# Two value products of 256 columns joined to one of 512 in a matmul-bound decoder trunk

## The chip, the cores and the metric

The kernel runs on one core of a Trainium2 chip. The metric is the device time of one execution in microseconds (us). Before the change it was run three times: median 2363.1, lowest 2362.75, highest 2363.84.

## The reference: what is computed

A decoder trunk of two layers on 512 tokens of width 1024. A layer is a half-step SwiGLU, then a token mixing of three kinds of attention side by side, then another half-step SwiGLU, each between RMS norms. Only the mixing is touched:

```python
u = _rmsnorm(h, mix_pre_g[l])
proj = u @ w_in[l]
q_sb, k_sb, v_sb, q_fx, k_fx, v_fx, f_logit, q_mem = jnp.split(proj, split_at, axis=-1)
o_sb = _stick_breaking_attention(heads(q_sb), heads(k_sb), heads(v_sb))
log_f = jax.nn.log_sigmoid((f_logit + b_forget[l]).astype(jnp.float32)).transpose(0, 2, 1)
o_fx = _forgetting_attention(heads(q_fx), heads(k_fx), heads(v_fx), log_f)
o_mem = _memory_attention(heads(q_mem), heads(k_mem), heads(v_mem))
g_sb, g_fx, g_mem = jnp.split(jax.nn.sigmoid(u @ w_gate[l] + b_gate[l]), 3, axis=-1)
merged = g_sb * (o_sb @ w_br_sb[l]) + g_fx * (o_fx @ w_br_fox[l]) + g_mem * (o_mem @ w_br_mem[l])
h = h + _rmsnorm(merged @ w_out[l], mix_post_g[l])
```

Stick-breaking ("sb") and forgetting ("fx", in the code "fox") attention have 8 heads of 64 each, so their values are 512 columns of `w_in` each: columns 1024 to 1535 and 2560 to 3071. The eight forget logits are the columns 3072 to 3079, directly behind the forgetting values. Forgetting attention adds the running sum of log_f to its scores.

## The kernel before, in words

**Three matmuls for one.** Every fp32 operand is split in a high part h (a rounding copy on ScalarE) and a low part l (a subtraction on VectorE), `split` (line 179). A product is then three matmuls, h·h, h·l and l·h: `mm3` (lines 203 to 207), or lines 1096 to 1098 in `vproj`. Weights come through a DMA on SP's queue into one of two "raw" buffers, and are split into one of four buffer pairs "wh" and "wl". Such a piece of weights is a `Unit` (line 232), of at most 128 x 1024 elements; `Unit.load` (line 252) fetches and splits it.

**The queue.** The big products are jobs in a `Queue` (line 350). A job is a list of units and a generator; each step of the generator emits one group of three matmuls. When a job starts, its units are loaded, and then those of the jobs behind it, until four units are counted (`load_ahead`, line 391). The attention heads are chains of small steps with waits between them (a score product, a softmax on ScalarE and VectorE, transposes on TensorE, a value product). `Queue.weave` (line 437) interleaves one head with steps of jobs, by an estimated time of the matmuls (`PE_US`, line 229), and a limit says up to which job the fillers of a head may go (lines 1474 and 1475). Between these, the framework orders instructions by their place in the program and by what is ready; the transposes and value products of a head are pinned behind what stands before them on TensorE.

**PSUM.** There are eight banks of 128 x 512: four of tag "z" (scores and transposes) and four of tag "mm" (all other products, among them a head's value product, line 1186). A bank is free again once its readers are done.

**Values.** A token tile is 128 tokens; there are four (NT), and eight 128-row blocks of the width (ND). For values the token tile is the stationary operand and the weight's columns are the moving one. Per layer `project_v` (line 1373) queues four jobs, each for the two pairs of heads in 256 columns:

- stick-breaking pairs 0 and 1, then pairs 2 and 3, and forgetting pairs 0 and 1: `v_half` (line 1345), two units of four blocks and 256 columns; it takes a bank for two token tiles, 256 columns each, and evacuates 512 columns at once.
- forgetting pairs 2 and 3 with the forget logits behind them: `v_gates` (line 1326), three units of up to three blocks and 264 columns; a bank for each token tile, evacuated as 256 columns of values and 8 of logits (line 1343).

The values lie in tiles of tag "v", six buffers, two tiles for each job. `forget_cumsum` (line 1285), queued behind forgetting's first k, transposes and sums the logits.

**The order of a layer's mixing.** The memory heads come first, with the first stick-breaking q, k and values as fillers; then eight stick-breaking heads, then eight forgetting heads (pairs 2, 3, 0, 1). The fillers are, in the queue's order: the next head pair's q and k, a merge (two gate products of the width, `pg`, and two branch products, `pb`), and the values of the pair after next (lines 1457 to 1467). `project_v(0, 2)` is queued in the first turn, `project_v(1, 2)` in the third and `project_v(1, 0)` in the fifth. In layer 0 these jobs run at 465 to 479 us, 556 to 571 us and 649 to 663 us of the trace; layer 1 has the same order some 1173 us later.

Of the kernel before, what the change touches and what calls it, by code (L numbers as in the profile page):

```python
# [9 lines left out]
F32 = mybir.dt.float32  # L10
# [8 lines left out]
P = 128  # L19
# [4 lines left out]
def kernel(  # L24
# [38 lines left out]
    nc = tc.nc  # L63
    _, S, D = x.shape
    M = mem.shape[1]
    L = w_in.shape[0]
    NT = S // P
    ND = D // P
    MT = M // P
    HD = 64  # L70
    NP = 4
    NH = 8
# [31 lines left out]
    def stile(shape, tag, name, dt=F32R):  # L104
        return sb.tile(shape, dt, tag=tag, bufs=BUFS[tag], name=name)
# [4 lines left out]
    def pbank(tag, name):  # L110
        return ps.tile([P, S], F32, tag=tag, bufs=4, name=name)
# [67 lines left out]
    def split(h_ap, l_ap, src, scale=None, later=False):  # L179

        if scale is None:
            both = [nc.scalar.copy(h_ap, src)]  # L182
            make = lambda: nc.vector.tensor_tensor(l_ap, src, h_ap.bitcast(F32), ALU.subtract)  # L183
        else:
            both = [nc.scalar.activation(h_ap, src, AF.Copy, scale=scale)]  # L185
            make = lambda: nc.vector.scalar_tensor_tensor(l_ap, src, scale, h_ap.bitcast(F32), ALU.mult, ALU.subtract)  # L186
        if later:
            return make
        both.append(make())
        if Q.pinned:  # L190
            for ins in both:
                tc.keep_in_program_order(ins)
# [10 lines left out]
    def mm3(pt, lh, ll, rh, rl, start, stop, free=False):  # L203

        nc.tensor.matmul(pt, lh, rh, start=start, stop=False, skip_group_check=free)  # L205
        nc.tensor.matmul(pt, lh, rl, start=False, stop=False, skip_group_check=free)  # L206
        nc.tensor.matmul(pt, ll, rh, start=False, stop=stop, skip_group_check=free)  # L207
# [14 lines left out]
    def quad_act(ts):  # L222

        return lambda k, c=FULL: (ts[k // 4][:, k % 4, 0, c], ts[k // 4][:, k % 4, 1, c])
# [4 lines left out]
    PE_US = 1 / 2370.0  # L229


    class Unit:


        def __init__(self, src, k0, nk, c0, ncol, name, scale=None):
            self.tags, self.place = ("wh", "wl"), "raw"
            self.src, self.k0, self.nk, self.c0, self.ncol, self.name, self.scale = src, k0, nk, c0, ncol, name, scale
            self.h = self.raw = None
# [5 lines left out]
        def fetch(self):  # L244
            if not self.waits():
                return
            Q.took(self.place, 1)
            self.raw = stile([P, self.nk, self.ncol], self.place, "raw_" + self.name, F32)
            nc.sync.dma_start(self.raw[:], self.src[self.k0 * P:(self.k0 + self.nk) * P, self.c0:self.c0 + self.ncol]
                              .rearrange("(k p) c -> p k c", p=P))  # L250
# [13 lines left out]
        def split_from(self, raw, **how):  # L264
            shape = [P, self.nk, self.ncol]
            if isinstance(self.tags, str):
                both = stile([P, 2] + shape[1:], self.tags, "w_" + self.name)
                self.h, self.l = both[:, 0], both[:, 1]
            else:
                self.h = stile(shape, self.tags[0], "wh_" + self.name)[:]  # L270
                self.l = stile(shape, self.tags[1], "wl_" + self.name)[:]
            return split(self.h, self.l, raw, scale=self.scale, **how)

    class BlockUnit(Unit):

# [68 lines left out]
    def wpair(src, ktiles, c0, name, scale=None):  # L344

        return [Unit(src, k, min(4, ktiles - k), c0, 256, f"{name}_{k}", scale) for k in range(0, ktiles, 4)]
# [116 lines left out]
    Q = Queue()  # L463
# [622 lines left out]
    def vproj(units, act, tiles, name):  # L1086

        pt = pbank("mm", name)
        for i, t in enumerate(tiles):
            o = pt[:, i * 256:(i + 1) * 256]  # L1090
            ts_ = slice(t * P, (t + 1) * P)
            for un in units:
                for k in range(un.nk):
                    ah, al = act(un.k0 + k)
                    first = i == 0 and un.k0 + k == 0
                    nc.tensor.matmul(o, ah[:, ts_], un.h[:, k], start=first, stop=False)
                    nc.tensor.matmul(o, ah[:, ts_], un.l[:, k], start=False, stop=False)
                    nc.tensor.matmul(o, al[:, ts_], un.h[:, k], start=False, stop=(i == 1 and un.k0 + k == ND - 1))  # L1098
                    yield 768 * PE_US
        return pt  # L1100
# [182 lines left out]
    FOX = (2, 3, 0, 1)  # L1283
# [24 lines left out]
    def mixing(l, src, ks, vs, rest, dst):  # L1308
# [4 lines left out]
        act = lambda k, c=FULL: quad_act(src.us)(k, c)  # L1313
        st, marks = {}, {}
# [11 lines left out]
        def v_gates(br, c, un):  # L1326

            st["fl"] = sb.tile([P, NT, NH], F32, tag="fl", bufs=1, name=f"fl{l}")
            for t in range(NT):
                if t % 2 == 0:  # L1330
                    vt = stile([P, 4, 4, HD], "v", f"v{l}_{br}_{c}_{t // 2}")
                    st.setdefault(("v", br, c), []).append(vt)
                pt = pbank("mm", f"pv{l}_{br}_{c}_{t}")
                for un1 in un:
                    for k in range(un1.nk):
                        kk = un1.k0 + k
                        ah, al = act(kk, slice(t * P, (t + 1) * P))
                        mm3(pt[:, :un1.ncol], ah, al, un1.h[:, k], un1.l[:, k], kk == 0, kk == ND - 1)
                        yield 3 * un1.ncol * PE_US
                e = 2 * (t % 2)  # L1340
                split(vt[:, e:e + 2, 0:4:3, :], vt[:, e:e + 2, 1:3, :],
                      pt[:, :4 * HD].rearrange("p (a e c) -> p a e c", a=2, e=2))
                nc.vector.tensor_copy(st["fl"][:, t], pt[:, 4 * HD:4 * HD + NH])

        def v_half(br, c, un):
            for i in range(NT // 2):

                vt = stile([P, 4, 4, HD], "v", f"v{l}_{br}_{c}_{i}")
                st.setdefault(("v", br, c), []).append(vt)
                pt = yield from vproj(un, act, (2 * i, 2 * i + 1), f"pv{l}_{br}_{c}_{i}")  # L1350
                split(vt[:, :, 0:4:3, :], vt[:, :, 1:3, :], pt[:].rearrange("p (a e c) -> p a e c", a=4, e=2))
# [21 lines left out]
        def project_v(br, p):  # L1373

            base = br * 1536 + 1024 + p // 2 * 2 * P
            if (br, p) == (1, FOX[0]):
                un = [Unit(w_in[l], k, min(3, ND - k), base, 2 * P + NH, f"v{l}_{br}_{p}_{k}")
                      for k in range(0, ND, 3)]
                Q.add(un, lambda: v_gates(br, p // 2, un))
            else:  # L1380
                un = wpair(w_in[l], ND, base, f"v{l}_{br}_{p}")
                Q.add(un, lambda: v_half(br, p // 2, un))

# [64 lines left out]
        for c in range(2):  # L1448
            un = wpair(w_in[l], ND, 3080 + c * 256, f"qm{l}_{c}")
# [3 lines left out]
        heads, fox = [(0, p) for p in range(NP)] + [(1, p) for p in FOX], []  # L1453
        project(*heads[0])
        project_v(*heads[0])
        marks[heads[0]] = len(Q.jobs)
        for i, (br, _) in enumerate(heads):
# [203 lines left out]
    for l in LAYERS:  # L1661
        i, mn = 3 * l, []
        ma = ffn(l, subs[i], ffn1_w_gate, ffn1_w_up, ffn1_w_down, subs[i + 1], f"a{l}", "v",
                 park[2 * l] if l else None, PLAN, lambda l=l, mn=mn: mem_norm(l, mn))
        rest = mem_kv(l, mn, *kvs[l])
        mb = mixing(l, subs[i + 1], *kvs[l], rest, subs[i + 2])
        if l == 0:
            Q.weave(begin(), ma["first"])
            more_constants()
        else:  # L1670
            for part, units in zip(mc["next"], (ma["early"][:2], ma["early"][2:])):
                part.extend(units)
            for un in ma["early"][2:]:
                un.place = "v"
            boundary(mc, mc["end"], ma["first"])
        boundary(ma, ma["end"], mb["first"])
        mb["run"]()
        mc = ffn(l, subs[i + 2], ffn2_w_gate, ffn2_w_up, ffn2_w_down, subs[i + 3], f"c{l}", "o", park[2 * l + 1], PLAN)
        for part, units in zip(mb["next"], (mc["early"][:2], mc["early"][2:])):
                part.extend(units)  # L1680
        boundary(mb, mb["end"], mc["first"])
# [25 lines left out]
```

## Time and profile before

| what | us |
|---|---|
| median of three runs | 2363.1 |
| the profiled execution | 2364.23 |
| span of its trace | 2362.5 |
| TensorE (PE) busy | 2341.4, 11719 matmuls |
| VectorE (DVE) busy | 1798.8 |
| ScalarE (ACT) busy | 1510.6 |

PE is the matmul part of TensorE, PEld its weight load, DVE VectorE, ACT ScalarE, POOL GpSimd, SP the engine that issues most transfers. An instruction is named by its line, its engine and the names of the tiles that it writes and reads ("pv<-wh_v,us_a": into a bank of values, from the value weights' high part and the normed activations). The profile's shares, groups and waits are of one execution. A matmul's record is the time from its start to its end, and the records of consecutive matmuls overlap; the distance of two starts tells what one costs in a stream.

### The profile page before, as it was taken

The numbers are of one execution on the slowest core, as the hardware profiler recorded it, in microseconds if no ns is written. First come the engines' busy times: TensorE is split into PE (matmuls) and PEld (weight loads), VectorE is DVE, ScalarE is ACT, GpSimd is POOL, SyncE is SP. The second block draws the span as 40 slices with busy tenths as digits, with TensorE's granted clock in tenths as the row PEclk, the third lists the DMA queues.
The fourth block names the chain that finished last, engine by engine and source line by source line (L and its number), as shares of the span: only waits on it lengthen the run. The fifth ranks groups of instructions, "written<-read, shape, count | busy, mean of one in ns | idle before, by whom it ended". The sixth has DMA issues, their size and how long they took to land.

```text
span 2362.5 us, 31122 instructions
## 1 busy us (share of the span) xinstructions
PE 2341.4 (99%) x11719; PEld 1980.5 (84%) x11719; DVE 1798.8 (76%) x2358; ACT 1510.6 (64%) x2305; POOL 75.4 (3%) x134
## 2 busy tenths in 40 slices
PE   9999999999999999999999999999999999999998
PEld 7788889888888888878888878888888888888887
DVE  8877877577777688878788778766767766887785
ACT  6777465576766556774556765655777665567744
POOL 0000000000111000000000000000001100000000
PEclk9999999999999999999999999999999999999999
DMA  5667454223323555674646665532323235566744
GB/s 205 183 178 216 147 190 139 81 83 88 90 72 107 188 188 162 194 187 154 221 131 195 200 178 167 198 108 72 95 76 99 72 124 188 171 186 175 220 140 143
DMA packets 299754, 354.98 MB, mean 150 GB/s; under 512 B 78266, under 2 KB 192978, under 8 KB 299604
## 3 DMA queue, kind: packets, MB, share of 16 engines
q1 hardware_dynamic: 299508, 352.97, 49.1%
q8 instruction: 92, 1.51, 0.3%
q14 instruction: 58, 0.48, 0.1%
q0 software_dynamic: 96, 0.03, 0.0%
HBM read 319.39 MB, written 16.78 MB: 142 GB/s over the span
## 4 chain that ended last, share of the span: by engine, by line
PE 85%; DVE 4%; DMA 4%; ACT 4%; issue 2%; SPq 0%; POOL 0%; DVEq 0%; ACTq 0%
PE pg L206 4%; PE pg L205 4%; PE pg L207 4%; PE pda L206 3%; PE pda L207 3%; PE pda L205 3%; PE pdc L206 2%; PE pdc L207 2%; PE pdc L205 2%; PE pb L206 2%; PE pb L207 2%; PE pb L205 2%; PE pq L206 1%; PE pq L205 1%; PE pk L207 1%
## 5 line engine op out<-in xcount | busy, mean ns | idle before, releaser
L205 PE MATMUL pg<-us_a,wh_wg 128*128 128x512 f32 x384 | 150.9, 393 | 0.0
L207 PE MATMUL pg<-us_a,wl_wg 128*128 128x512 f32 x384 | 149.8, 390 | 0.0
L206 PE MATMUL pg<-us_a,wh_wg 128*128 128x512 f32 x384 | 149.8, 390 | 0.0
L183 DVE TENSOR_TENSOR wl_da<-raw_da,wh_da 128x1024 fp32r<-128x1024 f32 x50 | 60.8, 1223 | 45.3 <-ACT wh_da L182 45.2
L183 DVE TENSOR_TENSOR wl_dc<-raw_dc,wh_dc 128x1024 fp32r<-128x1024 f32 x50 | 61.0, 1222 | 44.8 <-ACT wh_dc L182 44.7
L206 PE MATMUL pdc<-wl_dc,ahc 128*128 128x512 f32 x224 | 87.9, 392 | 1.2 <-DVE wl_dc L183 1.2
L206 PE MATMUL pda<-wl_da,aha 128*128 128x512 f32 x224 | 87.9, 392 | 0.9 <-DVE wl_da L183 0.8
L205 PE MATMUL pda<-wh_da,aha 128*128 128x512 f32 x224 | 86.8, 390 | 0.8 <-ACT wh_da L182 0.4
L205 PE MATMUL pdc<-wh_dc,ahc 128*128 128x512 f32 x224 | 86.8, 390 | 0.6 <-ACT wh_dc L182 0.4
L207 PE MATMUL pda<-wh_da,ala 128*128 128x512 f32 x224 | 87.3, 390 | 0.0
L207 PE MATMUL pdc<-wh_dc,alc 128*128 128x512 f32 x224 | 87.2, 390 | 0.0
L207 PEld LDWEIGHTS pg<-us_a,wl_wg 128*128 128x128 f32 x384 | 72.1, 188 | 15.2
L205 PEld LDWEIGHTS pg<-us_a,wh_wg 128*128 128x128 f32 x384 | 72.2, 188 | 14.1
L206 PEld LDWEIGHTS pg<-us_a,wh_wg 128*128 128x128 f32 x384 | 72.2, 188 | 14.1
L182 ACT CAST wh_da<-raw_da 128x1024 fp32r<-128x1024 f32 x50 | 52.0, 1051 | 41.6 <-DMA raw_da<-in_ffn_w_down_dram 12.8
L182 ACT CAST wh_dc<-raw_dc 128x1024 fp32r<-128x1024 f32 x50 | 52.1, 1048 | 38.3 <-DMA raw_dc<-in_ffn_w_down_dram 12.8
L186 DVE SCALAR_TENSOR_TENSOR wl_wg<-raw_wg,wh_wg 128x1024 fp32r<-128x1024 f32 x48 | 58.4, 1220 | 23.0 <-ACT wh_wg L185 23.0
L200 DVE SCALAR_TENSOR_TENSOR ga<-pg,bgate,ga 128x512 f32<-128x512 f32 x48 | 35.9, 747 | 48.8 <-ACT ga L199 48.8
L182 ACT CAST wh_uc<-raw_uc 128x1024 fp32r<-128x1024 f32 x44 | 46.4, 1054 | 35.3 <-PE pwc0g L207 8.3
L185 ACT ACTIVATE wh_wg<-raw_wg 128x1024 fp32r<-128x1024 f32 x48 | 50.6, 1057 | 25.5 <-PE pv L1098 11.4
L183 DVE TENSOR_TENSOR wl_uc<-raw_uc,wh_uc 128x1024 fp32r<-128x1024 f32 x44 | 53.7, 1220 | 16.1 <-ACT wh_uc L182 16.1
L182 ACT CAST wh_ua<-raw_ua 128x1024 fp32r<-128x1024 f32 x44 | 46.2, 1052 | 27.7 <-PE pwa1g L207 6.6
(647 smaller groups left out, 8049.2 us busy)
## 6 DMA issues: line engine op xcount, KB each, us to landing
raw_da<-in_ffn_w_down_dram SPq DMA_DIRECT2D x66, 512.0 KB, 4.8
raw_dc<-in_ffn_w_down_dram SPq DMA_DIRECT2D x66, 512.0 KB, 4.2
raw_ga<-in_ffn_w_gate_dram SPq DMA_DIRECT2D x52, 512.0 KB, 5.0
raw_ua<-in_ffn_w_up_dram SPq DMA_DIRECT2D x52, 512.0 KB, 4.4
raw_gc<-in_ffn_w_gate_dram SPq DMA_DIRECT2D x52, 512.0 KB, 4.1
raw_uc<-in_ffn_w_up_dram SPq DMA_DIRECT2D x52, 512.0 KB, 4.1
raw_wg<-in_w_gate_dram SPq DMA_DIRECT2D x48, 512.0 KB, 3.6
raw_wo<-in_w_out_dram SPq DMA_DIRECT2D x24, 512.0 KB, 3.6
```

The source lines that it names most:

```text
L182: both = [nc.scalar.copy(h_ap, src)]
L183: make = lambda: nc.vector.tensor_tensor(l_ap, src, h_ap.bitcast(F32), ALU.subtract)
L185: both = [nc.scalar.activation(h_ap, src, AF.Copy, scale=scale)]
L186: make = lambda: nc.vector.scalar_tensor_tensor(l_ap, src, scale, h_ap.bitcast(F32), ALU.mult, ALU.subtract)
L200: nc.vector.scalar_tensor_tensor(t, z, minus, t, ALU.max, ALU.add)
L205: nc.tensor.matmul(pt, lh, rh, start=start, stop=False, skip_group_check=free)
L206: nc.tensor.matmul(pt, lh, rl, start=False, stop=False, skip_group_check=free)
L207: nc.tensor.matmul(pt, ll, rh, start=False, stop=stop, skip_group_check=free)
```

## The change

Forgetting attention's two value jobs become one, `v_whole`, queued where the first of them was. It takes all four "mm" banks, one for each token tile, and goes through its four units (two blocks of 512 columns each) one by one: for each unit and token tile two blocks, six matmuls of 512 columns. With the last unit each bank is evacuated when its token tile is complete, as two halves of 256 columns into the four value tiles. The second forgetting value job is no longer queued. The forget logits are computed with the values of stick-breaking pairs 2 and 3, in `v_gates`, whose three units now have a second transfer for the 8 logit columns (`PairUnit`), since these do not lie behind those values in `w_in`.

```diff
+    class PairUnit(Unit):
+        def __init__(self, src, k0, nk, c0, n0, c1, n1, name):
+            super().__init__(src, k0, nk, c0, n0 + n1, name)
+            self.parts = ((0, c0, n0), (n0, c1, n1))
+        def fetch(self):
+            if not self.waits():
+                return
+            Q.took(self.place, 1)
+            self.raw = stile([P, self.nk, self.ncol], self.place, "raw_" + self.name, F32)
+            rows = self.src[self.k0 * P:(self.k0 + self.nk) * P]
+            for at, c, n in self.parts:
+                nc.sync.dma_start(self.raw[:, :, at:at + n], rows[:, c:c + n].rearrange("(k p) c -> p k c", p=P))
...
+        def v_whole(br, un):
+            pts = [pbank("mm", f"pv{l}_{br}_{t}") for t in range(NT)]
+            vts = {c: [stile([P, 4, 4, HD], "v", f"v{l}_{br}_{c}_{i}") for i in range(NT // 2)] for c in (1, 0)}
+            for c in vts:
+                st["v", br, c] = vts[c]
+            for un1 in un:
+                for t, pt in enumerate(pts):
+                    for k in range(un1.nk):
+                        kk = un1.k0 + k
+                        ah, al = act(kk, slice(t * P, (t + 1) * P))
+                        mm3(pt[:], ah, al, un1.h[:, k], un1.l[:, k], kk == 0, kk == ND - 1)
+                        yield 3 * S * PE_US
+                    if un1 is un[-1]:
+                        e = 2 * (t % 2)
+                        for c in vts:
+                            vt = vts[c][t // 2]
+                            split(vt[:, e:e + 2, 0:4:3, :], vt[:, e:e + 2, 1:3, :],
+                                  pt[:, c * 4 * HD:(c + 1) * 4 * HD].rearrange("p (a e c) -> p a e c", a=2, e=2))
...
-            if (br, p) == (1, FOX[0]):
-                un = [Unit(w_in[l], k, min(3, ND - k), base, 2 * P + NH, f"v{l}_{br}_{p}_{k}")
+            if (br, p) == (0, 2):
+                un = [PairUnit(w_in[l], k, min(3, ND - k), base, 2 * P, 3072, NH, f"v{l}_{br}_{p}_{k}")
                       for k in range(0, ND, 3)]
                 Q.add(un, lambda: v_gates(br, p // 2, un))
-            else:
+            elif (br, p) == (1, FOX[0]):
+                un = [Unit(w_in[l], k, 2, br * 1536 + 1024, S, f"v{l}_{br}_{k}") for k in range(0, ND, 2)]
+                Q.add(un, lambda: v_whole(br, un))
+            elif br == 0:
                 un = wpair(w_in[l], ND, base, f"v{l}_{br}_{p}")
                 Q.add(un, lambda: v_half(br, p // 2, un))
```

## The prediction, made before the result was known

> **What bounds the kernel now.** I read the page's busy table first, then the table of stretches over layer 0's token mixing, then the waits of TensorE, then its timeline.
>
> ```profile
> PE 2341.4 (99%) x11719; PEld 1980.5 (84%) x11719; DVE 1798.8 (76%) x2358; ACT 1510.6 (64%) x2305; POOL 75.4 (3%) x134
> PE 85%; DVE 4%; DMA 4%; ACT 4%; issue 2%; SPq 0%; POOL 0%; DVEq 0%; ACTq 0%
> ```
>
> TensorE is busy 99% of the span and makes 85% of the chain that ended last. A full row of nines may still hide a slow engine behind pipelined records, so the stage itself counts. The columns are the stretch, its length, then busy time and instructions of PE, PEld, DVE, ACT and POOL, the granted clock, DMA share, GB/s:
>
> ```profile
> 447.00:505.00 58.00, 58.00 (x322) 50.73 (x321) 40.77 (x61) 37.65 (x67) 4.76 (x7) 1.00 0.26 73
> 555.00:583.00 28.00, 28.00 (x186) 25.74 (x185) 19.26 (x34) 18.04 (x34) 0.20 (x1) 1.00 0.41 116
> 583.00:638.00 55.00, 55.00 (x267) 46.31 (x266) 42.14 (x62) 45.30 (x79) 6.72 (x11) 1.00 0.33 94
> 664.00:775.00 111.00, 111.00 (x572) 93.47 (x571) 81.30 (x163) 72.73 (x145) 13.54 (x25) 1.00 0.32 100
> ```
>
> In every stretch TensorE is busy for its whole length at clock 1.00, with VectorE at 69 to 77%. Over the whole span the longest waits of TensorE for another engine are these:
>
> ```profile
> PE utc L578 <- DVE nhc L484: 1.5, 1, 1.5
> PE utx L1597 <- DVE fx L1606: 1.3, 2, 0.9
> ```
>
> Neither tile belongs to the mixing; there TensorE never waits between 395 and 783 us. So in this stage time is what TensorE's instruction stream costs, and a change is worth the difference in that stream, plus any wait it creates where none is now.
>
> **The pace of a matmul.** The record of a matmul is its latency; the cost in a full stream is the distance of starts. First and last of four unbroken runs, 18, 45, 24 and 138 matmuls:
>
> ```profile
> 555.58 0.28 PE L205 MATMUL pv<-wh_v,us_a 128*128 128x264 f32 x1
> 557.64 0.28 PE L207 MATMUL pv<-wh_v,us_a 128*128 128x264 f32 x1
> ...
> 420.24 0.28 PE L1096 MATMUL pv<-wh_v,us_a 128*128 128x256 f32 x1
> 425.51 0.28 PE L1098 MATMUL pv<-wh_v,us_a 128*128 128x256 f32 x1
> ...
> 447.58 0.39 PE L205 MATMUL pg<-us_a,wh_wg 128*128 128x512 f32 x1
> 452.79 0.39 PE L207 MATMUL pg<-us_a,wl_wg 128*128 128x512 f32 x1
> ...
> 804.44 0.39 PE L205 MATMUL pwo<-wh_wo,ms 128*128 128x512 f32 x1
> 835.59 0.39 PE L207 MATMUL pwo<-wh_wo,ms 128*128 128x512 f32 x1
> ```
>
> 264 columns: 2.06 / 17 = 0.1212 us. 256 columns: 5.27 / 44 = 0.1198. 512 columns: 5.21 / 23 = 0.2265 and 31.15 / 137 = 0.2274. The last run is the nearest kin of the new product: token tiles stationary, a weight row of 512 moving, several banks taken in turn. Two matmuls of 256 cost 0.2396, one of 512 costs 0.2265: a fixed 13 ns per matmul is what the change can save.
>
> The Trainium skill, page "TensorE: Matmul & The Clock Gate", section "Back-to-back issue gap", gives N/2.4 + 2.5 ns for a warm matmul, so a fixed 2.5 ns; by that the sum below would be 0.25 us per layer, some 0.5 in all. The trace does not agree: 119.8 ns where the page's formula has 109.2 for 256 columns, and the measured paces decide.
>
> **The change, part by part, for one layer.**
>
> ```profile
> L1096 PE MATMUL pv<-wh_v,us_a x192: 277/283/364, 420.2 to 1835.8; 128*128 128x256 f32 x192
> L205 PE MATMUL pv<-wh_v,us_a x64: 280/283/367, 555.6 to 1743.2; 128*128 128x264 f32 x64
> ```
>
> One of the three lines of a product stands for a third: 3 x 64 / 2 = 96 matmuls of 264 per layer, and 3 x 192 / 2 = 288 of 256, which are three jobs of 96.
>
> 1. Forgetting attention's values: removed are 96 of 264 and 96 of 256, 11.64 + 11.50 = 23.14 us; added are 96 of 512, 21.74 us. **-1.39** (with the other run's 0.2274, -1.31).
> 2. The logits move to the stick-breaking job: 96 matmuls become 264 wide, 96 x 1.4 ns = **+0.13**.
> 3. Evacuation: two copies of 512 columns in the stick-breaking job become four of 256, and forgetting's four of 256 and two of 512 become eight of 256; the logit copies only move. From the shortest to the longest of them (ns, minimum, median, maximum):
>
> ```profile
> L182 ACT CAST v<-pv x20: 355/562/607, 428.7 to 1837.4; 128x512 fp32r<-128x512 f32 x12, 128x256 fp32r<-128x256 f32 x8
> L183 DVE TENSOR_TENSOR v<-pv,v x20: 409/674/685, 429.6 to 1838.6; 128x512 fp32r<-128x512 f32 x12, 128x256 fp32r<-128x256 f32 x8
> ```
>
> Four large ones go and eight small ones come: 8 x 0.355 - 4 x 0.562 = 0.6 us more on ScalarE, 8 x 0.409 - 4 x 0.674 = 0.6 on VectorE. VectorE has over 20% free in every stretch above: nothing on the path. If that cover were gone, the cost would be 0.6.
>
> 4. Loads: two units become three, and three plus two become four, seven units before and after with the same elements, so the splits cost the same. The three new transfers of 8 columns are issued on SP's queue ahead of the next weights. Nothing of this shape is in the trace; the nearest rows:
>
> ```profile
> raw_q<-in_w_in_dram SPq DMA_DIRECT2D x16, 512.0 KB, 4.0
> raw_v<-in_w_in_dram SPq DMA_DIRECT2D x2, 264.0 KB, 2.8
> ```
>
> 1024 rows land in 4.0 us, 256 in 2.8; a piece of at most 384 rows thus adds between 0 and 4.0 us to a unit's landing. The DMA engines are 26% busy there, and the weights are split several us ahead of their use, as TensorE's lack of waits shows. I take 0. It costs below zero nowhere, since no wait for these weights exists now.
>
> 5. Order. The job at 555.6 grows by 96 x (0.2265 - 0.1212) = 10.1 us and the later one vanishes, so that forgetting's first q and k and some gates run 10 us later:
>
> ```profile
> 576.28 0.39 PE L205 MATMUL pk<-us_a,wh_k 128*128 128x512 f32 x1
> ...
> 613.51 1.45 PE L1123 MATMUL pvs<-pts,v 128*128 128x256 f32 x8
> ...
> 616.54 0.39 PE L207 MATMUL pg<-us_a,wl_wg 128*128 128x512 f32 x1
> 616.77 0.39 PE L205 MATMUL pq<-us_a,wh_q 128*128 128x512 f32 x1
> ...
> 638.92 0.40 PE L1206 MATMUL zf<-causal,ident 128*128 128x128 bf16 x4
> ...
> 649.03 0.36 PE L1096 MATMUL pv<-wh_v,us_a 128*128 128x256 f32 x1
> ...
> 663.38 0.28 PE L1098 MATMUL pv<-wh_v,us_a 128*128 128x256 f32 x1
> ```
>
> The k product (24 matmuls from 576.3) ends at 581.7 and is first read at 638.9: 57 us of cover for 10. After the seventh stick-breaking head (613.5) only three gate matmuls were left before the q at 616.8, the point to which the planner lets that head's fillers go; the longer job leaves 10 us more there. Forgetting's first head, which was filled by the vanished job, gets those gates instead. Cost 0; if a head still ran out of fillers, it would wait as B below says.
>
> Without new waits: -1.39 + 0.13 = -1.26 us per layer, **-2.5 us** for two.
>
> 6. **Four banks at once.** The eight banks are four for scores and four for products ("mm"). The new product holds all four until its last unit; between 555.6 and its end an attention head wants one:
>
> ```profile
> 565.01 1.21 PE L1123 MATMUL pvs<-pts,v 128*128 128x256 f32 x7
> ...
> 606.26 1.25 PE L1137 MATMUL pts<-ident,ts 128*128 128x128 f32 x10
> ```
>
> This value product (pvs) can't start before the first bank is evacuated, so it slips some 12 us, behind the rest of the new product, which fills TensorE meanwhile. It releases one of two transposed-weight buffers, wanted again at 606: 26 us of cover. If the cover were gone, the head would cost its slip. Behind it on TensorE's queue stands the next q product, which needs a bank too.
>
> At the start, the banks come in the order in which the gate before released them: VectorE reads the last gate until 557.6 and the last branch product until 560.7:
>
> ```profile
> 556.84 0.75 DVE L200 SCALAR_TENSOR_TENSOR ga<-pg,bgate,ga 128x512 f32<-128x512 f32 x1 [1.38 <-ACT ga L199]
> 560.06 0.68 DVE L1431 TENSOR_TENSOR mg<-ga,pb 128x512 f32<-128x512 f32 x1
> ```
>
> The third bank is wanted after 12 matmuls, 555.6 + 2.7 = 558.3, and the fourth after 18 and the ten transposes (1.0 us) at 560.7: just in time, 0 to 0.2 us.
>
> At the end, the first bank's last matmul is 18 matmuls, 4.1 us, before the last one. A lag of evacuation up to 4.1 us is hidden; more is a wait. How long is the lag, from the last matmul of a token tile to the end of its subtraction? The second and the fourth tile of the job at 555.6:
>
> ```profile
> 562.37 0.29 PE L207 MATMUL pv<-wh_v,us_a 128*128 128x264 f32 x1
> ...
> 563.10 0.43 DVE L183 TENSOR_TENSOR v<-pv,v 128x256 fp32r<-128x256 f32 x1 [0.36 <-ACT v L182]
> ...
> 570.72 0.28 PE L207 MATMUL pv<-wh_v,us_a 128*128 128x264 f32 x1
> ...
> 577.94 1.20 DVE L186 SCALAR_TENSOR_TENSOR wl_wg<-raw_wg,wh_wg 128x1024 fp32r<-128x1024 f32 x1
> 579.70 1.23 DVE L183 TENSOR_TENSOR wl_wb<-raw_wb,wh_wb 128x1024 fp32r<-128x1024 f32 x1
> 580.92 0.41 DVE L183 TENSOR_TENSOR v<-pv,v 128x256 fp32r<-128x256 f32 x1
> ```
>
> The fourth tile was done at 571.0 and subtracted at 581.3, a lag of 10.3; the second was done at 562.7 and subtracted at 563.5, a lag of 0.9. The long lag stood behind the next head's softmax and two weight splits, and nobody waited for it. In the new job weights free one buffer per unit of 5.4 us, so fewer splits press, and the end falls where that softmax runs out. So the wait is between 0 and 10.3 - 4.1 = 6.2 us per layer; nearest is the short end, and I take **+0.4** for start and end together, +0.8 in all.
>
> Sum: -2.5 + 0.8 = **-1.7 us**. The profiled execution took 2364.2 us, 1.7 around the span of 2362.5; it would become 2362.5. The median of the runs is 1.1 lower, 2363.1, and becomes **2361.4**. A measurement of this kernel can tell about 0.2%, 4.7 us, from no change; the forecast lies inside that.
>
> **The rivals.**
>
> A. The full banks replace what is saved (slower). If evacuation keeps the long lag, TensorE waits up to 6.2 us per layer at the end of the product: 2363.1 - 2.5 + 12.4 = 2373.0. It decides from a lag of 4.1 + 1.26 = 5.4 us on. For it: two instructions per bank on each of two engines that work in order. Against it: the short lag above, and four matmul groups over which the four evacuations are spread. Chance 0.10.
>
> B. The moved job shifts the order elsewhere, and a few waits of the sort TensorE has now (at most 1.5 us each) come in: 1 to 3 us more than forecast, 2362.4 to 2364.4. For it: gates that ran beside the sticks now run beside forgetting's heads. Against: the stretch from 664 on has just that mix and no wait. Chance 0.16.
>
> C. The change does not do what it says: a 512 product that changes banks every six matmuls runs no faster than the halves, 2363.1 + 0.3 + 0.8 = 2364.2. Against: the run from 804.44, which changes banks every three. Chance 0.04.
>
> D. Weight loads lie bare between matmuls, and half as many are left:
>
> ```profile
> L205 PEld LDWEIGHTS pv<-wh_v,us_a x64: 187/188/190, 555.4 to 1743.1; 128*128 128x128 f32 x64
> ```
>
> 96 x 0.188 x 2 = 36 us, to 2327. The starts, 0.121 apart, are closer than one load lasts, so loads do lie under matmuls. Chance 0.01. The Trainium skill, same page, section "The mechanism", says that a weight load overlaps running matmuls only when it targets another row group; here loads of all 128 rows overlap, so the trace disagrees.
>
> **How the numbers follow.** The forecast (2360.0 to 2362.9: no wait to 1.2 us per layer) has 0.69, A 0.10, B 0.16, C 0.04, D 0.01. Faster by over 0.2% (under 2358.4) is D and a tail of the forecast: 0.03. Slower by over 0.2% (over 2367.8) is most of A and a tail of B: 0.11. Within: 0.86. The range takes the forecast, B and C, and the lower part of A: 2359.4 to 2366.0.
>
> **What would show it.** Starts of the new product's matmuls 0.2265 to 0.2274 apart, 96 per layer; the stick-breaking values 0.121 apart. The pvs now at 565 between some 577 and 581. No row "PE ... <- DVE v" or "<- ACT v" over 1 us among TensorE's waits, else A. TensorE's instruction count 11719 - 192 = 11527. Wrong would be a head that waits for its transposes, or a wait for the 8-column transfers in front of a weight split that TensorE then shares.

## The result, and the profile after

The changed kernel is slower: median 2370.5 us (six runs, 2367.8 to 2375.0) beside 2363.2 for the kernel before (six runs of it, 2359.5 to 2363.8). The ratio is 1.0033, 95% interval 1.0023 to 1.0042, so +7.3 us and outside the predicted range. The profiled execution took 2369.9 us. Behind the added code its line numbers are 16 to 39 higher than those of the kernel before: the head's value product pvs is L1139 now (was L1123), its transposes pts L1153 (L1137), the scores zs L1178 (L1162), the branch merge mg L1470 (L1431).

The page of the changed kernel, its busy times:

```profile
PE 2344.3 (99%) x11527; PEld 1972.5 (83%) x11527; DVE 1802.3 (76%) x2366; ACT 1510.4 (64%) x2313; POOL 74.4 (3%) x134
```

The 192 matmuls are gone (11527), and still TensorE is busy 2.9 us longer (2344.3 beside 2341.4, one execution each). The page hardly shows more. The stretches of layer 0 do (same columns as in the prediction; the new product, the two stretches behind it, and forgetting's heads):

```profile
556.00:584.00 28.00, 27.39 (x130) 22.57 (x129) 11.36 (x17) 11.74 (x22) 0.20 (x1) 1.00 0.39 113
584.00:612.00 28.00, 26.51 (x128) 20.82 (x127) 25.16 (x40) 21.63 (x42) 1.42 (x3) 1.00 0.19 57
612.00:638.00 26.00, 26.00 (x129) 21.99 (x127) 21.09 (x31) 23.26 (x40) 3.74 (x6) 1.00 0.30 92
664.00:775.00 111.00, 111.00 (x570) 93.39 (x569) 84.66 (x176) 72.03 (x148) 13.82 (x26) 1.00 0.28 91
```

Before the change TensorE was busy for the whole length of each of these. Now 0.61 us are missing during the new product and 1.49 us behind it. VectorE shows why to look there: 11.4 of 28 us busy during the product (41%), then 25.2 of 28 (90%). Work of the first stretch has slid into the second. The waits of TensorE over the whole span (total, count, longest) name three in the mixing that the kernel before did not have, and, ahead of the second layer's mixing, one that was 0.3 us there:

```profile
PE mt L1067 <- DVE mraw L1060: 1.6, 2, 1.1
...
PE pts L1153 <- ACT ts L1193: 1.5, 2, 0.7
...
PE pg L205 <- DVE k L183: 1.3, 2, 0.6
...
PE pv L205 <- DVE mg L1470: 0.9, 2, 0.6
```

The last three come twice, once per layer: a head's transposes (pts) that wait for its softmax, a gate (pg) that waits for a bank from a k product, and the new product's wait for its fourth bank (pv). The first one (mt, the transposes of the memory in layer 1) is taken up behind the experiments.

**Where the head lost its time.** TensorE's timeline of the changed kernel, from the scores of the sixth stick-breaking head (zs, pair 2, second head) to its transposes (pts):

```profile
567.56 1.45 PE L1178 MATMUL zs<-k,q 128*128 128x512 f32 x8
...
580.20 1.52 PE L1139 MATMUL pvs<-pts,v 128*128 128x256 f32 x8
...
582.95 0.39 PE L207 MATMUL pv<-wh_v,us_a 128*128 128x512 f32 x1
583.18 0.39 PE L205 MATMUL pq<-us_a,wh_q 128*128 128x512 f32 x1
...
591.10 0.33 PE L1153 MATMUL pts<-ident,ts 128*128 128x128 f32 x1 [0.73 <-ACT ts L1193]
```

The scores are ready at 569.0 and wait for 22 us until the head's transposes. The q product follows the last value matmul without a gap: no wait at the product's own end. ScalarE's timeline over the same time, first of the kernel before, then of the changed one (start, duration; in brackets the idle time before and what ended it):

```profile
566.50 0.58 ACT L1126 COPY ss<-pvs 64x512 f32<-64x512 f32 x1 [3.43 <-PE pvs L1123]
567.10 0.98 ACT L1167 ACTIVATE ts<-zs 128x512 f32<-128x512 f32 x2
```

```profile
571.10 1.05 ACT L182 CAST wh_k<-raw_k 128x1024 fp32r<-128x1024 f32 x1 [5.71 <-PE pv L207]
576.54 1.06 ACT L185 ACTIVATE wh_wg<-raw_wg 128x1024 fp32r<-128x1024 f32 x1 [4.38 <-PE pv L207]
577.90 0.37 ACT L182 CAST v<-pv 128x256 fp32r<-128x256 f32 x1 [0.30 <-PE pv L207]
...
581.76 0.58 ACT L1142 COPY ss<-pvs 64x512 f32<-64x512 f32 x1 [0.97 <-PE pvs L1139]
582.37 0.98 ACT L1183 ACTIVATE ts<-zs 128x512 f32<-128x512 f32 x2
```

The sixth head's softmax (ts<-zs) began at 567.10 before and begins at 582.37 now, 15.3 us later, while ScalarE sat idle for the last 2 of the 5.71 us and for all of the 4.38 us with the scores at hand. In both kernels it runs directly behind the copy of the fifth head's value product (ss<-pvs). That copy must wait for pvs, and pvs must wait for one of the four held banks. In the code the copy's target and the softmax tiles are buffers of one tag, "f32t", a ring of five buffers that are handed out in turn, in the order of the program:

```python
def tmp(name):
    return sb.tile([P, S], F32, tag="f32t", bufs=5, name=name)
...
s = tmp("s" + name)          # attend: the copy of a head's value product
nc.scalar.copy(s[r], pv[rl])
```

So a value product that slips holds up the softmax of the next head, which reads nothing of it. This is read off the order of the two instructions and the code; the experiments test it.

**How much it costs.** A yardstick that is steadier than the whole time: the mixing of a layer, from the first matmul of the memory queries (pqm) to the first of the output product (pwo). In layer 0 pqm starts at 376.41 and pwo at 804.44 before, at 377.35 and 808.18 after: 428.03 and 430.83 us. Layer 1 gives 428.03 and 430.50. Below, "mixing" is this stage, and "over pace" is the sum, over its matmuls, of what the distance to the next start exceeds that matmul's own pace (0.1198 us for 256 columns, 0.1212 for 264, 0.2265 for 512; for the others the median of the kernel before). Over pace are 2.12 us per layer before, and 6.17 and 5.85 after. So the changed kernel has 4.05 us more of waits and restarts in layer 0 (a restart is what the first matmuls after a wait take beyond their pace), against the 1.26 of the predicted saving: 4.05 - 1.26 = 2.79, where 430.83 - 428.03 = 2.80.

### The profile page after: what moved, and what is told of

The parts are those of the page before. It is cut to its first block, busy times and chain, and to the rows that moved or that the text cites. A ratio compares the mean times of both kernels' runs of the same rounds, so it can differ in the third digit from the quotient of the medians.

```text
span 2368.2 us, 30757 instructions
## 1 busy us (share of the span) xinstructions
PE 2344.3 (99%) x11527; PEld 1972.5 (83%) x11527; DVE 1802.3 (76%) x2366; ACT 1510.4 (64%) x2313; POOL 74.4 (3%) x134
## 3 DMA queue, kind: packets, MB, share of 16 engines
q8 instruction: 91, 1.49, 0.3%
## 4 chain that ended last, share of the span: by engine, by line
PE 87%; DVE 5%; ACT 3%; DMA 3%; issue 1%; SPq 0%; DVEq 0%; ACTq 0%
PE pg L206 3%; PE pg L205 3%; PE pg L207 3%; PE pda L206 3%; PE pda L207 3%; PE pda L205 3%; PE pdc L206 3%; PE pdc L207 3%; PE pdc L205 3%; PE pb L207 1%; PE pb L206 1%; PE pb L205 1%; PE pk L206 1%; PE pk L207 1%; PE pk L205 1%
```

## The experiments

T is the theory above: the ring. R1 and R2 are its rivals. R1 says that TensorE waits directly for the four held banks, at the start and the end of the new product; R2 lays the loss on the forget logits that moved. The copy has no part in either.

**1. copy_aside**: the changed kernel, but the fifth head's copy has a buffer outside the ring.

```diff
-        s = tmp("s" + name)
+        s = stile([P, S], "cs", "s" + name, F32) if name[0] == "s" and name[2:] == "_2_0" else tmp("s" + name)
```

> The changed kernel, with one edit: the buffer into which ScalarE copies half of the fifth stick-breaking head's value product (the head that waits for a bank) comes from another tag than the five-buffer ring that the next head's softmax uses. Banks, matmuls and order of the jobs stay. Theory T (the late value product holds its place in the ring, so the next head's softmax comes 15 us late on ScalarE and its transposes find TensorE waiting): the first softmax step of the sixth head moves from 582 back to about 569 us, the wait of the transposes for ScalarE (0.7 us per layer) and the splintered order behind it vanish, and most of the loss goes: 2361.5 to 2364, against 2363.2 before and 2370.5 after. What stays is the wait for the fourth bank at the start, 0.6 us in layer 0. Rival R1 (the four banks cost TensorE direct waits for banks, at start and end of the product): nothing is won, 2369 to 2371. Rival R2 (the moved logits and their transfers cost): nothing is won either.

Measured: 2364.9 us (11 runs) beside 2362.0 (33 runs), ratio 1.0014, 1.0005 to 1.0023; mixing 428.37 and 428.21. ScalarE and TensorE of this kernel:

```profile
567.01 0.98 ACT L1183 ACTIVATE ts<-zs 128x512 f32<-128x512 f32 x2 [2.81 <-PE zs L1178]
...
581.01 0.58 ACT L1142 COPY ss<-pvs 64x512 f32<-64x512 f32 x1 [0.97 <-PE pvs L1139]
```

```profile
561.46 0.50 PE L205 MATMUL pv<-wh_v,us_a 128*128 128x512 f32 x1 [0.54 <-DVE mg L1470]
...
579.45 1.52 PE L1139 MATMUL pvs<-pts,v 128*128 128x256 f32 x8 [0.30 <-DVE v L183]
583.80 1.25 PE L1153 MATMUL pts<-ident,ts 128*128 128x128 f32 x10
```

The copy is as late as ever (581.0), but the softmax no longer stands behind it (567.0), the transposes run at 583.80 in one piece, and both the wait of pts and the wait of pg for k are gone. What is left: the start wait, and now 0.30 at the value product itself. The matmuls of the two kernels are the same, so the mixing tells what the ring cost: 430.83 - 428.37 = 2.46 and 430.50 - 428.21 = 2.29 us per layer. T holds here, with a time 0.9 us above its range; both rivals expected no gain, and missed. R1 keeps a small part: the two waits that are left are direct waits for banks.

**2. two_banks and two_banks_again**: the same 512-column product in two passes, token tiles 0 and 1 and then 2 and 3, so that two banks are held instead of four.

```diff
-            pts = [pbank("mm", f"pv{l}_{br}_{t}") for t in range(NT)]
...
-            for un1 in un:
-                for t, pt in enumerate(pts):
+            for pair in ((0, 1), (2, 3)):
+                pts = [(t, pbank("mm", f"pv{l}_{br}_{t}")) for t in pair]
+                for un1 in un:
+                    for t, pt in pts:
```

> The changed kernel with the 512-column product in two passes over its four units: token tiles 0 and 1 through two banks, then 2 and 3, so that two product banks stay free for the heads. The same 96 matmuls of 512 per layer; the weights are held twice as long. Theory T and rival R1 both expect that the value product of the fifth head runs at its old place (about 566 us) and that no wait for a bank is left: the saving of 1.3 us per layer is seen, 2360 to 2362. Should the longer hold of the weights cost, there is a wait of the next q product for its weights, up to 2 us per layer. Rival R2 (logits): 2367 or more stays.

> The two-bank version once more. Its trace had the mixing 1.06 us shorter than before in each layer. Theory T expects the mixing at 427.0 us in both layers again, and a time 2 us below before, 5 to 8 below the changed kernel; chance elsewhere in the kernel moves single runs by some 3 us.

Measured: 2361.5 us, ratio 0.9997 (0.9988 to 1.0006), and the second time 2360.7 beside 2362.1, ratio 0.9993 (0.9984 to 1.0002). Mixing 426.97 in both layers of both runs, 1.06 less than before the change. TensorE of the first run:

```profile
565.79 1.45 PE L1139 MATMUL pvs<-pts,v 128*128 128x256 f32 x8
567.08 1.44 PE L1178 MATMUL zs<-k,q 128*128 128x512 f32 x8
...
582.65 1.25 PE L1153 MATMUL pts<-ident,ts 128*128 128x128 f32 x10
```

With two banks free the value product runs about where it did before the change, and TensorE waits for nobody in the mixing. The saving that the prediction worked out (1.26 per layer) is there, all but 0.2. It is 2.1 us in the whole, less than the total time can tell from no change; of all kernels tried this one has the shortest mixing, and only the stage in the trace says so.

**3. z_bank**: the changed kernel with all stick-breaking value products in a bank of the scores' tag "z", which the new product doesn't hold.

```diff
-        attend(pbank("mm", "pv" + name), j, vts, pj, wt, ot, name)
+        attend(pbank("z", "pv" + name), j, vts, pj, wt, ot, name)
```

> The changed kernel, with the value product of every stick-breaking head in a bank of the score tag instead of the product tag. The product of 512 still holds four banks. Theory T: the fifth head's value product runs at its old place, its copy too, so the next softmax is in time: 2361 to 2364; the wait for the fourth bank at the start (0.4 to 0.8 us per layer) stays. Rival R1: the waits at the end of the product for an evacuated bank stay as well, 2365 or more. Against it speaks that score banks may run short; then score products or transposes wait for a bank.

Measured: 2366.4 us, ratio 1.0022 (1.0013 to 1.0031); mixing 429.12 and 428.50. A miss: the fifth head is in time and its two waits are gone, but a new one came in at the first forgetting head (TensorE's waits of this kernel):

```profile
PE zf L1222 <- DVE ss L1143: 1.7, 2, 1.0
```

Eight heads' value products now take score banks, and forgetting's first scores wait for the last of them: 0.7 to 1.0 us, with its restart 1.15 and 0.89 over pace. The start wait stayed at 0.6 and 0.3. The trial was too broad for what it was to show; run 4 is its narrow form.

**4. z_one**: the same for the fifth head alone (one run).

```diff
-        attend(pbank("mm", "pv" + name), j, vts, pj, wt, ot, name)
+        attend(pbank("z" if name[2:] == "_2_0" else "mm", "pv" + name), j, vts, pj, wt, ot, name)
```

> The changed kernel with the value product of the fifth stick-breaking head alone in a bank of the score tag. Theory T: its copy and the next softmax are in time and forgetting's first head finds its four score banks free, so only the wait for the fourth bank at the start is left (0.4 to 0.8 us): mixing 427.4 to 427.9 us, against 428.0 before and 430.4 to 430.8 changed.

Measured: 2363.6 us beside one run of 2364.0 before; mixing 427.95 and 427.57. ScalarE of this kernel:

```profile
567.75 0.58 ACT L1142 COPY ss<-pvs 64x512 f32<-64x512 f32 x1 [3.66 <-PE pvs L1139]
568.36 0.98 ACT L1183 ACTIVATE ts<-zs 128x512 f32<-128x512 f32 x2
```

Copy and softmax are within 1.3 us of where they were before the change, without any edit of the ring. One wait is left in the mixing, the start (0.68 in layer 0). So the whole of the later loss in the mixing comes from this one value product being late, and the ring is how it spreads.

**5. logits_only**: the logits' move alone; forgetting's values stay two jobs of 256 columns.

```diff
-            elif (br, p) == (1, FOX[0]):
-                un = [Unit(w_in[l], k, 2, br * 1536 + 1024, S, f"v{l}_{br}_{k}") for k in range(0, ND, 2)]
-                Q.add(un, lambda: v_whole(br, un))
-            elif br == 0:
+            else:
```

> Only the move of the forget logits: they are computed with the values of stick-breaking pairs 2 and 3, with the extra 8-column transfers, and forgetting attention's values are two jobs of 256 columns as before. Theory T and R1: the 264-column matmuls only change places, so 2363.2 within 1 us. Rival R2: the loss is here, 2367 or more.

Measured: 2360.3 us beside 2362.0, ratio 0.9994 (0.9986 to 1.0003); mixing 428.32 and 428.41, so +0.29 and +0.38 (predicted +0.13). No wait of the three occurs. R2 falls.

**6. four_banks_264**: the kernel before, with its matmuls untouched, but its 264-column job goes unit by unit through four held banks. It separates holding four banks from the width of the matmul.

```diff
-            for t in range(NT):
...
-                pt = pbank("mm", f"pv{l}_{br}_{c}_{t}")
-                for un1 in un:
+            pts = [pbank("mm", f"pv{l}_{br}_{c}_{t}") for t in range(NT)]
...
+            for un1 in un:
+                for t, pt in enumerate(pts):
```

> The kernel before with one edit: the job of 264 columns (forgetting pairs 2 and 3) goes unit by unit through four banks that it holds at once, as the new product does; its matmuls are the same 96 of 264 columns, and the other forgetting job stays. No matmul is saved or added. Theory T: the banks are held for 11.6 us instead of 21.8, so the fifth head's value product slips by some 5 us from 565 and the next softmax with it; the fourth bank is wanted sooner (after 27 matmuls of 0.12 us) than the gate before releases it, so a wait of 1 to 1.5 us at the start. Together 1 to 3 us per layer, 2365 to 2368. If holding four banks did not matter and the 512-wide product itself did, 2362 to 2363 as before.

Measured: 2365.2 us, ratio 1.0011 (1.0002 to 1.0020); mixing 430.44 and 430.40, +2.4 per layer. TensorE's waits of this kernel:

```profile
PE pts L1137 <- ACT ts L1177: 1.8, 2, 0.9
PE pv L205 <- DVE mg L1431: 1.4, 2, 0.7
```

Two of the three waits, at the same places, without one new matmul. The value product slipped only from 565.0 to 569.5 here, and 4.5 us were enough for a wait of 0.9. It is the four held banks that cost; the width is not needed for it.

**7. four_banks_copy_aside**: run 6 with the copy of run 1 outside the ring (one run).

> The 264-column job through four held banks, and the fifth head's copy in a buffer outside the ring. With the banks held and the ring kept, a layer's mixing took 430.4 us, with a wait of 0.88 us for the fourth bank and one of 1.07 for the transposes. Theory T: the wait of the transposes goes and the one at the start stays: mixing 429.0 to 429.5 us in each layer. If the late value product itself, not the ring, delayed the softmax, 430.4 stays.

Measured: 2385.7 us beside 2364.0; mixing 438.85 and 438.51, 10.8 and 10.5 more than before the change. A miss, and the most instructive run. TensorE's wait, its timeline at the end of the job, and VectorE's:

```profile
PE pvs L1123 <- DVE fl L1343: 13.7, 2, 6.9
```

```profile
570.96 0.28 PE L207 MATMUL pv<-wh_v,us_a 128*128 128x264 f32 x1
578.09 2.68 PE L1123 MATMUL pvs<-pts,v 128*128 128x256 f32 x8 [6.85 <-DVE fl L1343]
580.57 0.63 PE L205 MATMUL pq<-us_a,wh_q 128*128 128x512 f32 x1
581.00 0.63 PE L206 MATMUL pq<-us_a,wh_q 128*128 128x512 f32 x1
...
584.28 0.39 PE L205 MATMUL pq<-us_a,wh_q 128*128 128x512 f32 x1
584.50 0.39 PE L206 MATMUL pq<-us_a,wh_q 128*128 128x512 f32 x1
```

```profile
576.60 0.42 DVE L183 TENSOR_TENSOR v<-pv,v 128x256 fp32r<-128x256 f32 x1
...
577.80 0.14 DVE L1343 COPY fl<-pv 128x8 f32<-128x8 f32 x1
```

The wait of pts went, as T said. But the softmax, now in time, ran on VectorE ahead of the evacuation, and the first bank was free only at 577.9, 6.7 us after the end of the job's last matmul. pvs and the q product behind it stood still for 6.85 us. That is rival A of the prediction, the lag of the evacuation, at its full price (6.2 us there). In run 6 the ring kept the softmax back until 571.7, and VectorE subtracted the first three banks from 568.85 on. The 512-column product lasts 10 us longer, so in run 1 the softmax was through before the first bank was complete. VectorE of copy_aside:

```profile
576.40 0.56 DVE L1192 TENSOR_TENSOR ts<-zs,ts 128x384 f32<-128x384 f32 x1
...
578.03 0.42 DVE L183 TENSOR_TENSOR v<-pv,v 128x256 fp32r<-128x256 f32 x1
```

T was right about what releases the softmax, and wrong that nothing else depended on its delay.

**8. The same kernels again** (changed_again five runs; before_look and changed_look one each).

> The changed kernel once more, beside the two-bank version on the same chip. The trace of its first run has the mixing 2.8 and 2.5 us longer than before in the two layers; theory T expects the same again: +5 to +7 us, 2367 to 2370, and the same three waits in each layer (fourth bank, transposes for ScalarE, gate product for k's evacuation).

> The kernel before once more, for its trace: the mixing at 428.0 us in both layers again, and the stages outside it, which hold no edited line, to see by how much they differ from run to run (1498.8 us in the first trace, 1498.4 and 1501.1 in the two of the changed kernel).

> The changed kernel a third time, for its trace: the mixing at 430.7 and 430.4 us, and the stages outside it between 1497 and 1501 us like those of the kernel before; if they lie 2 us or more above those of the kernel before every time, the change costs outside the mixing too.

changed_again: 2371.3 us beside 2362.1, ratio 1.0034 (1.0021 to 1.0048), mixing 430.65 and 430.40. before_look: 2361.5 us, mixing 428.03 twice, to the hundredth. changed_look: 2372.9 us, mixing 430.97 and 430.59. The stage repeats within some 0.3 us; the rest (the span less both mixings) doesn't: it is 1506.4 and 1503.7 us in two traces of the kernel before, and 1506.9, 1509.4 and 1509.6 in three of the changed one. So what was named as a sign that the change costs outside the mixing, 2 us or more above the kernel before every time, came in two of the three.

**What the mixing doesn't explain.** Both layers of mixing against the kernel before, and the difference of the medians, in us:

| kernel | mixing | medians | left over |
|---|---|---|---|
| changed | +5.3 | +7.3 | +2.0 |
| changed_again | +5.0 | +9.2 | +4.2 |
| copy_aside | +0.5 | +2.9 | +2.4 |
| z_bank | +1.6 | +4.3 | +2.7 |
| two_banks | -2.1 | -0.5 | +1.6 |
| two_banks_again | -2.1 | -1.4 | +0.7 |
| logits_only | +0.7 | -1.7 | -2.4 |
| four_banks_264 | +4.8 | +3.1 | -1.7 |

The intervals of the ratios are about 2 us to either side (3 for changed_again). Part of what is left over is chance, but changed_again's 4.2, z_bank's 2.7, copy_aside's 2.4 and the -2.4 of logits_only are more than that. None of these edits touches the rest of the span, but its waits are not the same. In layer 1 the memory's transposes (mt, behind a VectorE step) wait 1.6, 1.6 and 2.1 us in the three traces of the changed kernel, 0.3 and not at all in the two before; the output product (pwo, for the low part of its weights) waits 0.9, 1.4 and 1.4 us, against 0.1 and none. That these are the loss is not shown: two_banks has 1.9 and 0.9 us of the same waits, its second trace none and 0.9, and it is no slower than the kernel before. So 5 us of the 7 to 9 are placed and shown; where the other 2 to 4 lie stays open.

## Why the prediction was wrong

The sum to be explained is +2.8 and +2.5 us in the two layers' mixing in place of -0.86 each (-1.26 and +0.4). The rest of the miss, some 2 us of the whole time, lies outside the mixing and stays open.

- **Step 1, the paces: right.** The new product's first six matmuls start from 556.65 to 557.78 at 0.226, and the count is 11527. two_banks, where nothing waits, keeps 1.06 of the 1.26 per layer.
- **Step 2, the logits: right in kind**, +0.3 in place of +0.13.
- **Steps 3 to 5: right.** No wait for an evacuation of values, for a load or for forgetting's first k and q; from 612 on TensorE is full again.
- **Step 6, its end: no wait, but not for the step's reason.** It expected a short lag because fewer weight splits press. VectorE's subtractions of the new product's values:

```profile
580.82 0.42 DVE L183 TENSOR_TENSOR v<-pv,v 128x256 fp32r<-128x256 f32 x1 [0.44 <-ACT v L182]
...
592.36 0.76 DVE L183 TENSOR_TENSOR v<-pv,v 128x256 fp32r<-128x256 f32 x2
...
594.68 0.42 DVE L183 TENSOR_TENSOR v<-pv,v 128x256 fp32r<-128x256 f32 x1
```

  The first two banks are free at 580.0 and 581.2, some 2 us after their last matmuls, and pvs and q take them. The other two are free only at 593.1 and 595.1, a lag of 11 to 12 us behind the late softmax, as long as the 10.3 that the step had read; TensorE has no wait for them. Rival A's lag was there and cost nothing in this kernel, because it fell on the two banks that TensorE did not want yet; the step did not foresee that, so its outcome was luck. In run 7 the same lag fell on the first bank and cost 6.9.
- **Step 6, its start: mis-sized.** "0 to 0.2 us" is 0.61, with the restart 0.78 over pace, and 0.44 in layer 1. The step read from the kernel before when the branch merge was done. In the changed kernel a split of the product's own weights stands ahead of the merge. VectorE, then TensorE:

```profile
560.75 1.23 DVE L183 TENSOR_TENSOR wl_v<-raw_v,wh_v 128x1024 fp32r<-128x1024 f32 x1 [1.89 <-ACT wh_v L182]
561.89 0.68 DVE L1470 TENSOR_TENSOR mg<-ga,pb 128x512 f32<-128x512 f32 x1
```

```profile
562.62 0.50 PE L205 MATMUL pv<-wh_v,us_a 128*128 128x512 f32 x1 [0.61 <-DVE mg L1470]
```

- **Step 6, the slipped value product: this is the step that failed.** The slip itself came as predicted (580.2, within 577 to 581). What failed is the "26 us of cover". The step asked which buffer the value product releases. It did not ask what stands behind the instruction that reads the value product: on ScalarE its copy came next, and the five-buffer ring put the following head's softmax behind that copy. The transposes slid from 581.7 to 591.1, and the fillers hid all of it but 0.73. The rest came in its train, since the steps of two heads now fell together: transposes splintered between the matmuls of k, and later a gate that wanted the bank of a k product whose evacuation stood behind the softmax. TensorE and then VectorE:

```profile
591.18 0.48 PE L206 MATMUL pk<-us_a,wh_k 128*128 128x512 f32 x1
591.52 0.44 PE L1153 MATMUL pts<-ident,ts 128*128 128x128 f32 x2
...
608.79 0.50 PE L205 MATMUL pg<-us_a,wh_wg 128*128 128x512 f32 x1 [0.64 <-DVE k L183]
```

```profile
608.04 0.69 DVE L183 TENSOR_TENSOR k<-pk,k 64x512 fp32r<-64x512 f32 x1
```

  Over pace in layer 0, restarts included: 0.90 for the wait of pts, 0.80 for that of pg, 0.28 at the next transposes, 0.78 at the start, and 1.3 in gaps of less than 0.2 each, most of them where the kind of matmul changes. Together 4.05.
- **The rivals.** What came is B's symptom ("a head that waits for its transposes"), at two and a half times its highest price: B went to 1.5 us per layer above the forecast, and it is 3.66 (2.80 + 0.86). C and D did not come. The range was too narrow mainly for one reason: the price of a full slip was put at nothing without the list of what waits behind it. Without that price, in copy_aside, the time is 2364.9, inside the range.

## What to carry to other kernels

When a step slips, look not only at who reads its result and which buffer it releases, but at what stands behind the instruction that evacuates it on its engine, and which later tiles come from the same ring of buffers. A saving on a full engine is safest if it holds no more of a shared resource than before: the same 512-column matmuls over two banks kept nearly all of the gain that four banks turned into a loss. And an accidental delay can protect something, so a wait that is taken away is to be followed to what then comes first.

## What the runs showed of the hardware

In run 7 the product behind the long wait did not start at its pace. Its first matmuls of 512 columns start 0.43 us apart (581.00 - 580.57), then some 0.23 (584.50 - 584.28 = 0.22). The stretches of that kernel show why in the granted clock, the third number from the right:

```profile
573.00:574.00 1.00, 0.00 (x0) 0.00 (x0) 1.00 (x2) 1.00 (x4) 0.00 (x0) 0.93 0.85 297
574.00:575.00 1.00, 0.00 (x0) 0.00 (x0) 1.00 (x3) 0.52 (x3) 0.00 (x0) 0.50 0.00 0
...
584.00:584.50 0.50, 0.50 (x3) 0.42 (x2) 0.00 (x0) 0.00 (x0) 0.06 (x1) 0.90 0.00 0
```

A mean of 0.93 in the first row puts the drop to one half at 573.9, 2.6 us after the last matmul ended (571.24), and 0.90 in the last one puts the return at 584.1, 6.0 us after work came back (578.09). In layer 1 of this run the drop came 4.9 us after the last matmul ended (1753.39 to 1758.28) and the return 4.8 us after work came back (1760.27 to 1765.11). In layer 0 the wait of 6.9 us cost some 2.9 us more in slow matmuls: eight of 512 columns at 0.2 each, and the value product, whose start stands 2.48 ahead of the next product's in place of 1.29. The Trainium skill, page "TensorE: Matmul & The Clock Gate", section "What's actually happening", has the clock halved after an idle window of about 3.4 us and full again after about 3.4 us of work, in windows that run free. The half clock lasted 10.24 and 6.83 us in the two layers, three and two times 3.41, which agrees with such windows. But the first drop came after less idleness, 2.6 us, and both returns took longer, 6.0 and 4.8 us.

In one other trace a shorter wait was followed by the same. In changed_look the memory's transposes waited 2.07 us (1496.38 to 1498.45), and the granted clock was one half from 1499.46 to 1502.87, when products were already running again: nine starts there took 3.64 us (1499.40 to 1503.04) in place of 9 x 0.2265 = 2.04. The same wait of 1.15 and 1.31 us in the other two traces of the changed kernel left the clock at 1.00.
